# Twenty loads at the end of layer 1's attention begun by POOL in place of SP

## The chip, the cores and the metric

The program runs on one core of a Trainium2 chip. Its five engines each work through a queue of their own, in the order in which the program was built: PE (TensorE, matrix products), DVE (VectorE), ACT (ScalarE), POOL (GpSimd) and SP (SyncE, which here only begins transfers). Semaphores order the engines among each other. The metric is the device time of one execution in microseconds (us), given as the median of three runs.

## What is computed

Two decoder layers over 1024 positions of width 1024. Layer 1 ends its mixer part like this (cut from the reference):

```python
o_mix = forgetting_attention(q, k_sh, v_sh, dcum)      # 12 heads of 64
o_mem = memory_attention(q_mem, mem, mem_norm[l], w_mem_kv[l])   # 4 heads of 64
x = x + jnp.concatenate([o_mix, o_mem], axis=-1) @ w_o[l]        # 1024 x 1024
x = x + conv_ffn(rms_norm(x, ffn_norm[l]), w_up[l], conv_w[l], conv_b[l], w_down[l])
```

The change sits between the attention of layer 1 and the product with `w_o[1]`.

## The kernel before

Every large product is computed with two-part operands: a value is split into a rounded part (`hi`, written by ACT, line 173) and the rest (`lo`, written by DVE, line 174), and three products are summed (`mm3`, lines 249 to 251).

Layer 1's attention is written by `attention`. Its units are a head and a half `c` of the positions (512 of them). A unit's scores are made by PE (`score`, line 392, into `psa`), masked by DVE (line 422), exponentiated by ACT (line 435) and scaled by DVE (line 482). Then, step by step, PE turns 128-wide blocks (line 512, into `psb`), ACT and DVE split them into `pt` (lines 523 and 526), and PE multiplies them with the values (line 536). ACT copies the finished unit to `ob` (line 628) and SP stores it to the DRAM tensor `o` (line 630), both parts apart. Between these steps the projections of the queries and keys of later heads are computed; they read the layer's input from four `hT` buffers.

When both heads of a pair (`kt`, eight of them) are stored for one `c`, `operand` loads the pair's 128 rows of `o` (line 595), POOL adds the two parts (line 596), and ACT and DVE split the sum into `oT`, the left operand of the output projection. There are 16 operands. In the order of the program they are (c, kt) = (0,0), (1,0), (0,1), (1,1), (0,6), (1,6), (0,2), (1,2), (0,3), (1,3), (0,7), (1,7), (0,4), (1,4), (0,5), (1,5); "operand 7" below is the seventh of these. `oT` takes the four `hT` buffers, so no operand can be split before the projections have read their last input of that half. Once, at the start of the last unit, `load_block` loads the first half of the columns of `w_o[1]` in four pairs of `kt` (`load_rows`, line 282), each split into `wh` and `wl` (lines 173 and 174 again).

All these loads, 16 and 4, and the projections' weights before them, land in `wr`, which has three buffers: `wraw` gives the next one, and a load into it waits until the split of the one before has read it. Behind the attention `out_proj` runs over the columns in two halves `n` and the rows in eight tiles `t`; tiles 0 to 3 need the operands of c = 0, tiles 4 to 7 those of c = 1, and each takes `kt` in the order 0, 1, 2, 3, 4, 6, 7, 5. It accumulates in `psb`, of which there are four; DVE adds the sum to `x` (line 1290). The second half of `w_o[1]` is loaded there, by SP.

The order on each engine in layer 1's attention is made by a scheduler: it takes the operations by the order of the program, as their inputs and buffers come free by its own estimate of the times. So a transfer that is put on another queue also changes the order of the other engines. Once built, the order is fixed, and an engine whose next instruction waits does nothing else.

Of the kernel before, what the change touches and what calls it, by code (L numbers as in the profile page):

```python
# [18 lines left out]
P = 128  # L19
# [3 lines left out]
KT = D // P  # L23
CH = 512
# [15 lines left out]
def f32(ap):  # L40
    return ap.bitcast(F32)
# [93 lines left out]
class Trunk:  # L135
# [137 lines left out]
        self.split(raw, hi, lo)  # L273
        return lambda kt: (hi[:, kt, :], lo[:, kt, :])

    def load_rows(self, w, k0, nk, cols, gcol=None, pool=None):

        width = sum(n for _, n in cols)
        raw = self.wraw([P, nk, width])
        o = 0  # L280
        for c0, n in cols:
            self.nc.sync.dma_start(raw[:, :, o:o + n], w[k0 * P:(k0 + nk) * P, c0:c0 + n].rearrange("(k p) n -> p k n", p=P))
            o += n
        if pool is None:
            hi, lo = self.whl([P, nk, width])
        else:
            hi, lo = (self.sb(pool, [P, nk, width], F32R, n, KT // nk) for n in ("bh", "bl"))
        if gcol is None:
            self.split(raw, hi, lo)
        else:  # L290
            for k in range(nk):
                g = gcol[:, k0 + k:k0 + k + 1]
                self.nc.scalar.activation(hi[:, k, :], raw[:, k, :], AF.Identity, scale=g)
                self.nc.vector.scalar_tensor_tensor(lo[:, k, :], raw[:, k, :], g, f32(hi[:, k, :]), ALU.mult, ALU.subtract)
        return hi, lo

    def load_block(self, w, cols, gcol=None, step=2, pool=None):
        tiles = [self.load_rows(w, k0, min(step, KT - k0), cols, gcol, pool) for k0 in range(0, KT, step)]

        def at(kt, c0, n):  # L300
            hi, lo = tiles[kt // step]
            return hi[:, kt % step, c0:c0 + n], lo[:, kt % step, c0:c0 + n]
        return at
# [254 lines left out]
    def attention(self, ap, l, od, units, work, spare, lead=4, lag=2, lead_work=2):  # L558
# [30 lines left out]
        def operand():  # L589

            if not oT:
                oT.extend(self.hpair() for _ in range(2))
            c, kt = whole.pop(0)
            raw = self.wraw([P, 2, CH])
            self.nc.sync.dma_start(raw, od[c][:, kt * P:(kt + 1) * P, :].rearrange("s p q -> p s q"))
            self.nc.gpsimd.tensor_tensor(raw[:, 0], raw[:, 0], raw[:, 1], ALU.add)  # L596
            self.split(raw[:, 0], oT[c][0][:, kt, :], oT[c][1][:, kt, :])

# [3 lines left out]
        def run(k, slot):  # L602
            for f in later.pop((k, slot), ()):
                f()

        def advance():
            nonlocal total
            total -= 1
            if next(work[0][1], 0) == 0:
                done.add(work.pop(0)[0])  # L610

        def begin(k, it):
            if it["load"]:
                while not set(it["u"]["needs"]) <= done:
                    advance()
                it["u"]["load"]()
            self.score(it)
            after(k + 1, "max", lambda: self.maximum(ap, it))
            after(k + 1, "exp", lambda: self.exponent(ap, it))
            if "norm" in it:  # L620
                after(k + 2, "norm", lambda: self.normalise_all(it["u"], *it["norm"]))

        def finish(k, u):
            h, c = u["at"]

            def out():
                ot = self.sb(ap, [P, CH], F32, "ob", 2)
                self.nc.scalar.activation(ot, u["o"], AF.Copy)
                for i in range(2):
                    self.nc.sync.dma_start(od[c][i, h * HD:(h + 1) * HD, :], ot[i * HD:(i + 1) * HD, :])  # L630
                halves.append((c, h // 2))
                if halves.count((c, h // 2)) == 2:
                    whole.append((c, h // 2))
            after(k + 1, "exp", out)

        first = min(it["at"] for it in items)
        for k in range(first, len(steps) + lag + 4):
            st = steps[k] if 0 <= k < len(steps) else None
            run(k, "max")
            if st:  # L640
                self.turn_p(ap, st)
                self.upper_p(ap, st)
            run(k, "exp")
            if st:
                self.lower_p(st)
            run(k, "norm")
            while items and items[0]["at"] <= k:
                begin(k, items.pop(0))
            if k < 0 and lead_work and items:
                for _ in range(lead_work):  # L650
                    if work:
                        advance()
            if st and k < n_fill:
                owed += max(total, 0) / (n_fill - k)
                while owed >= 1 and work:
                    owed -= 1
                    advance()
            if 0 <= k - lag < len(steps):
                for part in range(len(steps[k - lag]["t"])):
                    self.value(steps[k - lag], part)  # L660
                if steps[k - lag]["end"]:
                    finish(k, steps[k - lag]["u"])
            if not work and whole and k % 4 == 0:
                operand()
            if k == units[-1]["start"]:
                w_o = self.load_block(self.a["w_o"][l], [(0, CH)])
        while whole:
            operand()
        assert not work and not later
# [1320 lines left out]
```

## Time and profile before

| | us |
|---|---|
| median of 3 runs | 2552.12 |
| lowest, highest | 2549.92, 2553.2 |
| profiled execution, its own time | 2546.43 |
| its span | 2544.6 |
| PE busy in the span | 2455.0 (96%) |
| DVE, ACT, POOL busy | 1823.9 (72%), 1340.3 (53%), 791.3 (31%) |

The profile is one execution. Its times count from the start of the span; 1.8 us of its own time lie outside. A line of the timeline has the start, the length, the engine, the line of the kernel, what is written from what, and, in brackets, how long the engine had been idle and what ended that. "SPq" is an issue on SP's queue: its length is that of the issue, not of the transfer. In the chain of waits, a "DMA" piece is the part of a transfer that the chain waited for. POOL's operations before layer 1's attention ended lie in other stages; from 1607 to 1845 us it does nothing but the 16 additions of line 596. The products of the first half `n` of the output projection begin at 1787.8 us.

### The profile page before, as it was taken

The numbers are of one execution on the slowest core, as the hardware profiler recorded it, in microseconds if no ns is written. First come the engines' busy times: TensorE is split into PE (matmuls) and PEld (weight loads), VectorE is DVE, ScalarE is ACT, GpSimd is POOL, SyncE is SP. The second block draws the span as 40 slices with busy tenths as digits, with TensorE's granted clock in tenths as the row PEclk, the third lists the DMA queues.
The fourth block names the chain that finished last, engine by engine and source line by source line (L and its number), as shares of the span: only waits on it lengthen the run. The fifth ranks groups of instructions, "written<-read, shape, count | busy, mean of one in ns | idle before, by whom it ended". The sixth has DMA issues, their size and how long they took to land.

```text
span 2544.6 us, 35639 instructions
## 1 busy us (share of the span) xinstructions
PE 2455.0 (96%) x12306; PEld 2052.6 (81%) x12306; DVE 1823.9 (72%) x3074; ACT 1340.3 (53%) x2553; POOL 791.3 (31%) x714
## 2 busy tenths in 40 slices
PE   7899999988999999999999999999999999999998
PEld 7788888776878888888889888887777888888886
DVE  5648787676477877879765468878476778778765
ACT  5338787686254544544454356767244444444443
POOL 1235555485135564540000000000234455551000
PEclk9999999999999999999999999999999999999999
DMA  8473333344323332358235467665622233238533
GB/s 248 140 218 91 92 109 104 88 140 158 118 76 103 104 111 96 104 182 290 93 124 165 144 182 203 188 180 176 221 89 87 94 106 112 95 104 307 170 95 115
DMA packets 302700, 357.68 MB, mean 141 GB/s; under 512 B 37960, under 2 KB 183224, under 8 KB 302520
## 3 DMA queue, kind: packets, MB, share of 16 engines
q1 hardware_dynamic: 302520, 355.41, 44.1%
q8 instruction: 97, 1.59, 0.3%
q14 instruction: 83, 0.68, 0.1%
HBM read 245.55 MB, written 109.78 MB: 140 GB/s over the span
## 4 chain that ended last, share of the span: by engine, by line
PE 79%; DVE 5%; ACT 4%; DMA 3%; POOL 2%; issue 2%; SPq 1%; POOLq 0%; ACTq 0%; DVEq 0%
PE psa L249 12%; PE psa L250 12%; PE psa L251 12%; PE psb L251 9%; PE psb L249 9%; PE psb L250 9%; PE psa L392 5%; PE psb L512 4%; PE psb L536 4%; ACT pt L523 1%; DVE pt L526 1%; ACT ps L435 1%; DVE ps L422 1%; DMA qq<-qd 1%; PE psb L1322 1%
## 5 line engine op out<-in xcount | busy, mean ns | idle before, releaser
L173 ACT ACTIVATE wh<-wr 128x512 fp32r<-128x512 f32 (+2 forms) x240 | 181.8, 761 | 311.4 <-PE psb L251 146.7
L1764 DVE SCALAR_TENSOR_TENSOR v<-u,cw,v 128x1023 f32<-128x1023 f32 (+1 forms) x176 | 275.2, 1564 | 68.7 <-ACT v L1762 68.5
L174 DVE TENSOR_TENSOR wl<-wr,wh 128x512 fp32r<-128x512 f32 (+2 forms) x232 | 222.9, 963 | 121.3 <-ACT wh L173 120.6
L526 DVE TENSOR_TENSOR pt<-psb,pt 128x512 fp32r<-128x512 f32 (+2 forms) x380 | 244.4, 660 | 70.0 <-ACT pt L523 68.6
L1762 ACT ACTIVATE v<-u,cw 128x1024 f32<-128x1024 f32 x88 | 109.6, 1245 | 310.0 <-DVE u L1751 296.9
L523 ACT ACTIVATE pt<-psb 128x512 fp32r<-128x512 f32 (+2 forms) x380 | 212.9, 575 | 106.2 <-PE psb L512 70.0
L536 PE MATMUL psb<-pt,vv 128*128 128x512 f32 (+2 forms) x864 | 244.0, 361 | 11.9 <-DVE pt L526 7.3
L213 POOL TENSOR_TENSOR rs<-ss,consts 128x1 f32<-128x1 f32 x44 | 25.5, 582 | 675.9 <-DVE ss L211 467.2
L249 PE MATMUL psa<-hT,wh 128*128 128x512 f32 x560 | 219.1, 392 | 5.3 <-DVE u L1725 5.3
L251 PE MATMUL psa<-hT,wl 128*128 128x512 f32 x560 | 218.5, 390 | 0.2 <-DVE wl L174 0.2
L250 PE MATMUL psa<-hT,wh 128*128 128x512 f32 x560 | 218.5, 390 | 0.0
L392 PE MATMUL psa<-kk,qq 128*128 128x512 f32 (+4 forms) x792 | 178.8, 344 | 16.0 <-DMA qq<-qd 5.0
L536 PEld LDWEIGHTS psb<-pt,vv 128*128 128x128 f32 x864 | 144.5, 190 | 33.0 <-DVE pt L526 12.5
L435 ACT ACTIVATE ps<-ps,stat 128x128 f32<-128x128 f32 (+1 forms) x192 | 147.3, 770 | 31.9 <-DVE stat L422 31.6
L422 DVE CUSTOM_DVE_ANT_0 ps<-psa,caub 128x128 f32<-128x128 f32 (+1 forms) x192 | 138.9, 751 | 32.5 <-PE psa L392 29.8
L249 PE MATMUL psb<-hT,wh 128*128 128x512 f32 x384 | 156.6, 408 | 1.2 <-ACT wh L173 0.9
L392 PEld LDWEIGHTS psa<-kk,qq 128*128 128x128 f32 x792 | 121.9, 192 | 38.7 <-DVE stat L422 14.7
L251 PE MATMUL psb<-hT,wl 128*128 128x512 f32 x384 | 151.8, 395 | 0.8 <-POOL wl L174 0.8
L250 PE MATMUL psb<-hT,wh 128*128 128x512 f32 x384 | 151.0, 393 | 0.0
L512 PE MATMUL psb<-consts,ps 128*128 128x128 f32 x928 | 146.6, 276 | 4.2 <-DVE pt L526 3.4
L596 POOL TENSOR_TENSOR wr<-wr 128x512 f32<-128x512 f32 x16 | 21.6, 1353 | 411.5 <-DMA kd<-st 243.7
L1666 POOL TENSOR_TENSOR ws<-wr 128x512 f32<-128x512 f32 x44 | 77.5, 1761 | 216.2 <-DMA wr<-in_w_up_dram 175.7
(310 smaller groups left out, 6830.3 us busy)
## 6 DMA issues: line engine op xcount, KB each, us to landing
wr<-in_w_up_dram SPq DMA_DIRECT2D x88, 512.0 KB
wr<-gd SPq DMA_DIRECT2D x154, 256.0 KB
gd<-v SPq DMA_DIRECT2D x88, 256.0 KB
gd<-gs SPq DMA_DIRECT2D x66, 256.0 KB
o<-ob SPq DMA_DIRECT2D x128, 128.0 KB
wr<-o SPq DMA_DIRECT2D x32, 512.0 KB
hT<-in_w_down_dram SPq DMA_DIRECT2D x64, 256.0 KB
qd<-st SPq DMA_DIRECT2D x56, 256.0 KB
```

Of the source, the lines that this page charges most:

```text
L173: nc.scalar.activation(hi, src, AF.Copy)
L174: (low or nc.vector).tensor_tensor(lo, src, f32(hi), ALU.subtract)
L249: mm(out, lh, rh, start=first, stop=False, skip_group_check=more)
L250: mm(out, lh, rl, start=False, stop=False, skip_group_check=more)
L251: mm(out, ll, rh, start=False, stop=last, skip_group_check=more)
L392: nc.tensor.matmul(out, w, rhs, start=b not in banks[:i], stop=b not in banks[i + 1:])
L435: nc.scalar.activation(p, p, AF.Exp, bias=st[:, 0, ii:ii + 1], scale=-1.0, accum_out=st[:, 1, ii:ii + 1])
L512: nc.tensor.transpose(tp[0:kb, x:x + P], br["pt"][ii][:, o:o + kb], self.ident)
L523: self.nc.scalar.activation(st["hi"], st["src"], AF.Copy)
L526: self.nc.vector.tensor_tensor(st["lo"], st["src"], f32(st["hi"]), ALU.subtract)
L536: self.nc.tensor.matmul(u["o"][:, iis[0] * P:iis[0] * P + w], br["v"](j), t[:, x:x + w], start=st["begin"] and first and i == 0, stop=st[" ...
L1764: nc.vector.scalar_tensor_tensor(v[:, d:], u[:, :S - d], cw[:, tap, i:i + 1], v[:, d:], ALU.mult, ALU.add)
```

## The change

`load_rows` and `load_block` take a queue, which is SP's if none is given. The operand loads and the four loads of the first half of `w_o[1]` are begun by POOL:

```diff
-    def load_rows(self, w, k0, nk, cols, gcol=None, pool=None):
+    def load_rows(self, w, k0, nk, cols, gcol=None, pool=None, queue=None):
...
-            self.nc.sync.dma_start(raw[:, :, o:o + n], w[k0 * P:(k0 + nk) * P, c0:c0 + n].rearrange("(k p) n -> p k n", p=P))
+            (queue or self.nc.sync).dma_start(raw[:, :, o:o + n], w[k0 * P:(k0 + nk) * P, c0:c0 + n].rearrange("(k p) n -> p k n", p=P))
...
-            self.nc.sync.dma_start(raw, od[c][:, kt * P:(kt + 1) * P, :].rearrange("s p q -> p s q"))
+            self.nc.gpsimd.dma_start(raw, od[c][:, kt * P:(kt + 1) * P, :].rearrange("s p q -> p s q"))
...
-                w_o = self.load_block(self.a["w_o"][l], [(0, CH)])
+                w_o = self.load_block(self.a["w_o"][l], [(0, CH)], queue=self.nc.gpsimd)
```

Nothing else is edited. On POOL, at the end of the attention, the loads now stand among the additions. The part from operand 6 (`wr_17468`) on, with the weight pairs (`wr_17485` to `wr_17503`) and operands 7 to 10 (`wr_17544`, `wr_17581`, `wr_17592`, `wr_17597`), lines with + are new on this engine:

```order
 L596 TENSOR_TENSOR wr_17468<-wr_17468 128x512
+L282 DMA wr_17491<-in_w_o_dram 128x2x512
+L282 DMA wr_17497<-in_w_o_dram 128x2x512
+L282 DMA wr_17503<-in_w_o_dram 128x2x512
+L595 DMA wr_17544<-o_0_13658 128x2x512
+L595 DMA wr_17581<-o_1_13659 128x2x512
 L596 TENSOR_TENSOR wr_17544<-wr_17544 128x512
+L595 DMA wr_17592<-o_0_13658 128x2x512
 L596 TENSOR_TENSOR wr_17581<-wr_17581 128x512
+L595 DMA wr_17597<-o_1_13659 128x2x512
 L596 TENSOR_TENSOR wr_17592<-wr_17592 128x512
```

Before, POOL had the additions alone. Now each load from operand 9 on stands behind the addition of the operand two places earlier; so it goes on to the end.

On ACT, the copies of operand 6 and of the first three weight pairs (`wh_17487`, `wh_17493`, `wh_17499`) move forward, among the softmax of a later unit (`ps_2736`):

```order
 L628 ACTIVATE ob_17145<-psb_17085 128x512
+L173 ACTIVATE hT_17090<-wr_17468 128x512
 L523 ACTIVATE pt_17170<-psb_17165 128x512
+L173 ACTIVATE wh_17487<-wr_17485 128x1024
 L523 ACTIVATE pt_17186<-psb_17181 128x512
 L523 ACTIVATE pt_17202<-psb_17197 128x512
+L173 ACTIVATE wh_17493<-wr_17491 128x1024
+L173 ACTIVATE wh_17499<-wr_17497 128x1024
+L435 ACTIVATE ps_2736_17135,stat_17134<-ps_2736_17135,stat_17134 128x640
+L435 ACTIVATE ps_2736_17135,stat_17134<-ps_2736_17135,stat_17134 128x768
 L523 ACTIVATE pt_17217<-psb_17214 128x256
```

Before, the copy of operand 6 stood some 30 rows later, ahead of the first weight pair's. Operand 5's copy (`hT_17088<-wr_17407`) moves in the same way, to the place ahead of `pt_17008`, a unit earlier.

On DVE, near the end of the attention, the split of the second weight pair (`wl_17494`) now stands where that of the first (`wl_17488`) stood:

```order
+L526 TENSOR_TENSOR pt_17458<-psb_17455,pt_17458 128x256
 L450 TENSOR_SCALAR stat_17338<-stat_17338 128x4
-L174 TENSOR_TENSOR wl_17488<-wr_17485,wh_17487 128x1024
+L174 TENSOR_TENSOR wl_17494<-wr_17491,wh_17493 128x1024
 L451 RECIPROCAL stat_17338<-stat_17338 128x4
-L526 TENSOR_TENSOR pt_17458<-psb_17455,pt_17458 128x256
+L174 TENSOR_TENSOR wl_17500<-wr_17497,wh_17499 128x1024
 L482 TENSOR_SCALAR ps_2777_17339<-ps_2777_17339,stat_17338 128x640
```

The first pair's and operand 6's splits have gone forward on this engine too, and the third pair's now stands ahead of the last unit's scalings, not behind them.

## Rows read from the trace of the kernel before

**Rows 1.** The page's first part: busy time, share, instructions of each engine.

```profile
PE 2455.0 (96%) x12306; PEld 2052.6 (81%) x12306; DVE 1823.9 (72%) x3074; ACT 1340.3 (53%) x2553; POOL 791.3 (31%) x714
```

**Rows 2.** Stretches: length, busy us of PE, PEld, DVE, ACT, POOL, clock, DMA, GB/s.

```profile
1740.00:1750.00 10.00, 9.42 (x60) 7.52 (x58) 9.36 (x25) 8.30 (x20) 0.00 (x0) 1.00 0.79 235
1750.00:1760.00 10.00, 9.38 (x54) 7.77 (x53) 8.70 (x24) 7.30 (x18) 1.29 (x1) 1.00 0.59 181
...
1770.00:1780.00 10.00, 6.78 (x35) 4.68 (x36) 9.56 (x19) 6.47 (x12) 0.00 (x0) 0.96 0.29 90
1780.00:1790.00 10.00, 8.70 (x36) 6.37 (x35) 9.04 (x12) 6.13 (x11) 2.59 (x2) 0.70 0.70 227
1790.00:1800.00 10.00, 9.58 (x41) 7.52 (x42) 2.90 (x4) 2.83 (x5) 5.18 (x4) 1.00 0.79 238
1800.00:1810.00 10.00, 8.28 (x36) 6.08 (x35) 3.83 (x6) 2.82 (x5) 6.11 (x4) 1.00 0.78 263
```

**Rows 3.** Whom PE waited for, 1600 to 1860: us in total, times, longest.

```profile
PE psb L536 <- DVE pt L526: 5.0, 8, 1.1
PE psb L249 <- ACT hT L173: 2.1, 3, 1.5
...
PE psa L392 <- DMA qq<-qd: 0.8, 1, 0.8
```

**Rows 4.** PE's timeline in the output projection (start, length, instruction, idle before).

```profile
1802.86 0.50 PE L249 MATMUL psb<-wh,hT 128*128 128x512 f32 x1 [1.48 <-ACT hT L173]
...
1807.06 0.50 PE L249 MATMUL psb<-wh,hT 128*128 128x512 f32 x1 [0.24 <-ACT hT L173]
```

**Rows 5.** The chain of waits that ended last, at the tail: start, length, what.

```profile
1792.23 4.67 DMA wr<-o
...
1800.20 3.42 DMA wr<-o
```

**Rows 6.** POOL's timeline: addition 7, and 14 with 15.

```profile
1785.71 1.30 POOL L596 TENSOR_TENSOR wr<-wr 128x512 f32<-128x512 f32 x1 [16.97 <-DMA wr<-o]
...
1803.75 2.59 POOL L596 TENSOR_TENSOR wr<-wr 128x512 f32<-128x512 f32 x2 [1.60 <-DMA wr<-o]
```

**Rows 7.** The page's third part: DMA queues, packets, MB, share of 16 engines.

```profile
q1 hardware_dynamic: 302520, 355.41, 44.1%
```

**Rows 8.** Line 595 alone: issue in ns (least, median, most), first and last start.

```profile
L595 SPq DMA_DIRECT2D wr<-o x16: 359/370/586, 1615.5 to 1803.6; - x16
```

**Rows 9.** SP's timeline: the issues of operands 7 to 10.

```profile
1780.84 9.14 SPq L595 DMA_DIRECT2D wr<-o x4
```

**Rows 10.** DVE's timeline: splits of operands and weights, a block, a burst of scalings.

```profile
1731.71 0.68 DVE L174 TENSOR_TENSOR hT<-wr,hT 128x512 fp32r<-128x512 f32 x1
...
1742.09 0.69 DVE L174 TENSOR_TENSOR hT<-wr,hT 128x512 fp32r<-128x512 f32 x1 [0.29 <-ACT hT L173]
...
1775.81 1.22 DVE L174 TENSOR_TENSOR wl<-wr,wh 128x1024 fp32r<-128x1024 f32 x1
...
1777.04 0.39 DVE L526 TENSOR_TENSOR pt<-psb,pt 128x256 fp32r<-128x256 f32 x1
1777.35 2.33 DVE L482 TENSOR_SCALAR ps<-ps,stat 128x640 f32<-128x640 f32 x4
1779.59 1.22 DVE L174 TENSOR_TENSOR wl<-wr,wh 128x1024 fp32r<-128x1024 f32 x1
...
1787.83 1.76 DVE L174 TENSOR_TENSOR hT<-wr,hT 128x512 fp32r<-128x512 f32 x1
```

**Rows 11.** ACT's timeline: what now stands behind a copy, and a weight pair's copy.

```profile
1737.97 0.60 ACT L523 ACTIVATE pt<-psb 128x512 fp32r<-128x512 f32 x1 [0.16 <-PE psb L512]
...
1748.43 1.27 ACT L523 ACTIVATE pt<-psb 128x512 fp32r<-128x512 f32 x2 [0.50 <-PE psb L512]
...
1753.88 0.82 ACT L435 ACTIVATE ps<-ps,stat 128x640 f32<-128x640 f32 x1
...
1772.97 1.05 ACT L173 ACTIVATE wh<-wr 128x1024 fp32r<-128x1024 f32 x1
```

## What I expect of it, and why

> **What bounds the kernel now.** The page's first part comes first: TensorE (PE) is busy for 96% of the span [rows 1], so a change gains only where PE waits, and loses wherever it makes PE wait. Then the stretches of ten microseconds around the place of the change [rows 2]: from 1740 to 1760 us PE is busy for 9.4 of 10, from 1770 to 1780 only for 6.78, from 1780 to 1790 its granted clock is 0.70 on the mean (1 is 2.4 GHz, 0.5 is 1.2), and until 1810 us it still has gaps. VectorE (DVE) is busy for 9.56 and 9.04 of 10 us from 1770 to 1790, so until then DVE sets the pace, not a transfer. The list of waits says the same [rows 3]: between 1600 and 1860 us PE waited 5.0 us for DVE's `pt` and 2.1 us, in three pieces, for ACT's `hT`, the operands of the output projection; its only wait for a transfer is 0.8 us for a `qq`, which is not among the transfers that move. The two larger pieces of the 2.1 us that matter are PE's stops before 1802.86 (1.48 us) and 1807.06 us (0.24) [rows 4], for the thirteenth and the fifteenth operand. After the second, PE has no gap to speak of for the rest of the first half of the projection. So the end of this stage is the arrival of operand 15; the chain of waits runs over two of the tail's loads [rows 5], POOL's additions [rows 6] and ACT's copy.
>
> **What the change removes.** 16 operand loads and 4 weight loads leave SP's queue. Since PE waited 0.8 us for a transfer in 260 us [rows 3], nothing late is freed by that: the stores and query loads that stood behind them were in time. I cost the emptier SP at nothing; what covers it is that PE and DVE are full there, and without that cover it is worth the 0.8 us.
>
> **What it adds: the loads on POOL.** All transfers of the kernel's data run over one hardware queue [rows 7], and no row shows one begun by POOL, so its price needs bounds. Below: SP's price, 0.37 us to issue [rows 8], and 3.42 us to landing, the faster of the two tail loads in the chain [rows 5]. Above: an issue as long as POOL's own addition over the same tile, 1.30 us [rows 6], and the slower landing plus the longer issue, 4.67 + 0.93 = 5.6 us. I take the middle of the issue, 0.83 us, and the middle of the landings (4.05 us) plus the 0.46 us by which the issue is longer: L = 4.5 us from the start of the issue to the data. A price below SP's own I leave out: the same bytes go over the same 16 engines.
>
> By the Trainium skill (DMA: Bandwidth & Descriptors, Latency and other measured facts) the first byte comes some 0.6 us after the start from the sync queue and some 1 us from POOL's; L would then be an estimated 4.45 us and the sum below 2.5 instead of 2.8 us. No run here shows it.
>
> **What it moves (1): the prefetch depth at the tail.** Before, SP issues an operand's load as soon as one of three buffers is free, so three are in flight, and a pair of additions takes 4.8 us: addition 7 starts at 1785.71 us, addition 15 ends at 1803.75 + 2.59 = 1806.34 us [rows 6]. After, loads and additions stand in one queue, and the order reads load n+1, addition n, load n+2, addition n+1. Load n+2 cannot begin before addition n is done, although its buffer may be free: two are in flight, not three. A pair then costs L + 1.3 us, 5.8 us at L = 4.5. From the end of addition 7 to that of addition 15 there are four pairs.
>
> **What it moves (2): where the tail begins.** Operand 7 takes the buffer of the second weight pair. Before, its load was issued at 1780.84 us [rows 9], when DVE's second `wl` had ended (1779.59 + 1.22) [rows 10]. After, operand 6 and the first weight pair stand earlier on DVE, and the second `wl` follows where the first stood: that ended at 1775.81 + 1.22 = 1777.03 us, then a `pt` of 0.39 and a `wl` of 1.22 give 1778.6 us [rows 10], 2.2 us earlier, if nothing before it is delayed.
>
> **What it moves (3): three places where ACT can now stand.** ACT and DVE work in a fixed order, and the new order puts copies of loads between the softmax work. Operand 5's load may go when DVE has split operand 3 (1731.71 + 0.68) [rows 10], at 1732.4 us; it lands at 1736.9, POOL adds operand 4 first (till 1737.2), then it (till 1738.5), ACT copies till 1739.15. The `pt` behind it started at 1737.97 us before [rows 11]: 1.2 us late. Operand 6 waits for operand 2's split, which ended at 1742.09 + 0.69 = 1742.78 [rows 10] and now near 1744.0; landed 1748.5, added 1749.8, copied 1750.4, while the `pt` behind it started at 1748.43 [rows 11]: 2.0 us late. The third weight pair takes operand 6's buffer (split by 1751.1), lands at 1755.6 us and is copied (1.05 us) by 1756.7; the exponential behind it started at 1753.88 [rows 11]: 2.8 us late, of which 2.1 us are two weight copies that only moved. This is one delay that grows, not three. DVE was idle for 0.64 + 1.30 = 1.9 us from 1740 to 1760 us [rows 2], which takes part of it. I take S = 1.5 us left at operand 7, and as ends 0 (POOL as quick as SP) and 3 us (all of the largest place).
>
> **The sum.** Addition 15 ends at 1778.6 + S + 5 x (L + 1.3). With S = 1.5 and L = 4.5 that is 1809.1 us against 1806.34: **2.8 us later**. PE then stands some 2 us more before operand 15, and the rest follows unchanged, since PE has no gap behind it to make it up. The profiled execution (2546.43 us, span 2544.6) would become 2549.2; the median of the runs is 2552.12, and the same 2.8 us on it give **2554.9 us**. Ends: L = 3.42 and S = 0 give 1802.2, 4.1 us earlier, of which PE can use the 2.1 us that it waited for operands and perhaps 2 more from DVE work that has left the full stretch: 2548. L = 5.6 and S = 3 give 1816.1, 9.8 us later: 2562.
>
> One row speaks for a further price. The split of operand 7 at 1787.83 us took DVE 1.76 us where others take 0.69 [rows 10], beside one of POOL's additions: the two engines hinder each other. The Trainium skill (SBUF — State Buffer, Who interferes with whom) states that POOL cannot write a transfer's descriptors while DVE runs an operation in a two-port mode, which `tensor_scalar`, the kernel's scaling by 1/sum, can enter. The scalings come in bursts of four, 2.33 us for the long ones [rows 10]. By that rule the third weight load, released just ahead of a burst of short ones, would come about half such a burst later, S would be some 1.2 us larger and the sum 4.0 us; without it, 2.8.
>
> **Rivals.** A difference of 0.2%, 5.1 us, is about what a measurement of this kernel can tell from no change.
> - *The POOL load is dear* (slower by over 0.2%). Place: the alternation of loads and additions at the tail. The sum rises by 5 us for each microsecond of L, and by S; 5.1 us are passed near L = 4.9 with S = 2, which is the slower landing with an issue of 0.6 us. It would give 2558 to 2562. For it: both upper ends are ordinary rows, and longer stops of PE may bring its clock down as after the gaps of 1770 to 1780 us; a stretch like that from 1780 to 1790 us costs up to 3 us [rows 2]. Against: the faster landing. Chance 0.33.
> - *The POOL load is as cheap as SP's and the earlier splits pay* (faster by over 0.2%). The 2.1 us of operand waits go, DVE is relieved of operand 6 and the first weight pair in its full stretch, and PE keeps its clock from 1780 to 1790 us (up to 3 us): 2547. For it: DVE is the bound there. Against: two in flight instead of three, and the work that left that stretch went into one that is nearly as full. Chance 0.08.
> - *It does not reach the end.* The order changes, but the earlier start pays for the slower pairs (L near 4.2, S near 1: 0.8 us later): 2552 to 2553. This belongs to "no change" with the forecast.
>
> **How the numbers follow.** The forecast with the third rival 0.59, the slower rival 0.33, the faster 0.08. The likeliest is the forecast, 2554.9. The range from 2548 to 2562 is that of the two ends of the sum and leaves about 0.1 on either side.
>
> **What would show it.** In the trace after: the length of POOL's row of a load (0.83 by me) and the time from its start to the addition (L). Additions 9, 11, 13 and 15 should be near 5.8 us apart, and PE's stop before operand 15 near 2 us where it was 0.24. ACT should stand before the copies of operands 5 and 6. The prediction is wrong if POOL's issue costs as little as SP's, if three loads turn out to be in flight, if DVE loses more than 3 us before 1770 us to the copies that now stand ahead, or if PE's clock from 1780 to 1790 us comes out otherwise, which no row of before decides.

## The result, and the profile after

The changed kernel takes 2567.64 us (median of 4 runs, 2567.15 to 2571.34), the kernel before 2551.02 (4 runs) beside it: a ratio of 1.0071 with an interval of 1.0060 to 1.0083, or 18 us of 2551 (the two medians alone are 16.6 us apart). The forecast was 2.8 us; the time lies above its range, 2548 to 2562. The profiled execution took 2571.34 us (span 2569.5), the slowest of the four; that of before, 2546.43 us, was a quick one.

Two executions cannot be compared by their clock times as they stand. The first row of line 628 (`ob<-psb`), at 1492.32 us before, starts at 1496.61 after, and the rows up to 1572 us keep that distance within 0.07 us. The first load that the change moves comes at 1615.5 us [rows 8], so 4.29 us is the distance between the two executions. **Late** below always means: later than the same row of before, less this distance, which is taken anew for each kernel. Up to the end of attention it is good to about 1.5 us: e11 below, whose order is that of before up to operand 6, is 0.5 us late at 1590 us and 1.6 at the end of attention. It compares single executions, and behind attention it differs from the measured times by up to 3.7 us (e7).

The stretches of ten microseconds of the kernel after, against [rows 2] (length; busy us of PE, PEld, DVE, ACT, POOL; clock; DMA share; GB/s):

```profile
1750.00:1760.00 10.00, 7.01 (x41) 5.16 (x41) 9.43 (x25) 7.36 (x18) 4.11 (x5) 1.00 0.83 257
1760.00:1770.00 10.00, 5.39 (x15) 4.18 (x16) 4.35 (x8) 4.88 (x9) 0.00 (x0) 0.70 0.68 191
...
1810.00:1820.00 10.00, 7.58 (x31) 5.91 (x30) 2.62 (x4) 1.89 (x3) 6.22 (x6) 0.93 0.84 256
1820.00:1830.00 10.00, 6.84 (x23) 5.06 (x23) 2.67 (x4) 1.26 (x2) 3.40 (x4) 0.84 1.02 407
```

Two holes are new. In the first, from 1750 to 1770 us, where PE was busy for 18.5 of 20 before, it is busy for 12.4, and the granted clock falls to 0.70 on the mean (0.5, the lower level, from 1764.5 to 1770). In the second, from 1810 to 1830, PE stands for 5.6 of 20 while the transfer engines fill up (0.84, then 1.02 and 407 GB/s). PE's stops from 1790 to 1810 us are for the most part those that before had from 1770 to 1790, moved along. Whom PE waited for from 1600 to 1880 us, against [rows 3]:

```profile
PE psb L249 <- ACT hT L173: 5.6, 2, 3.2
PE psa L392 <- DMA qq<-qd: 5.5, 2, 5.3
PE psb L536 <- DVE pt L526: 4.6, 5, 2.0
PE psb L512 <- DVE ps L482: 3.8, 4, 2.7
```

The wait for DVE's `pt`, the largest before, is no larger. Three grew: the one for an operand (`hT`), which the prediction spoke of, the one for a query (`qq`), which it had set aside with 0.8 us, and the one for DVE's scalings (`ps`, 0.3 before), which it did not price (more on that one with e10 and e13 below).

The query's story on SP's timeline (issues), after:

```profile
1749.51 3.24 SPq L1033 DMA_DIRECT2D qd<-st  x2
...
1755.01 3.97 SPq L1502 DMA_DIRECT2D qq<-qd  x2
```

POOL's, in the same microseconds:

```profile
1737.83 0.72 POOL L595 DMA_DIRECT2D wr<-o  x1 [81.71 <-DVE hT L174]
1739.03 0.72 POOL L595 DMA_DIRECT2D wr<-o  x1 [0.48 <-DVE hT L174]
...
1751.10 0.72 POOL L595 DMA_DIRECT2D wr<-o  x1 [4.26 <-ACT pt L523]
1752.07 0.72 POOL L282 DMA_DIRECT2D wr<-in_w_o_dram  x1 [0.25 <-DVE hT L174]
...
1756.82 0.73 POOL L282 DMA_DIRECT2D wr<-in_w_o_dram  x1
1758.67 0.72 POOL L282 DMA_DIRECT2D wr<-in_w_o_dram  x1 [1.12 <-DVE hT L174]
```

And PE's:

```profile
1764.43 1.62 PE L392 MATMUL psa<-kk,qq 128*128 128x512 f32 x4 [5.32 <-DMA qq<-qd]
```

The query is stored to DRAM by `qd<-st` and read back by `qq<-qd`; PE waits for it. Beside that pair POOL now moves operand 6 and three pairs of weights, 512 KB each. Before, SP began operand 6 and the first weights behind the queries and the stores (SP's timeline of before):

```profile
1763.43 0.59 SPq L595 DMA_DIRECT2D wr<-o  x1
1764.12 12.15 SPq L282 DMA_DIRECT2D wr<-in_w_o_dram  x3
```

The tail, SP's timeline of before and, in the second fence, of after (the eight loads of the residual rows, `x<-xd`, 512 KB each):

```profile
1800.20 3.72 SPq L595 DMA_DIRECT2D wr<-o  x3
...
1805.20 4.46 SPq L1519 DMA_DIRECT2D x<-xd  x8
```

```profile
1815.30 4.11 SPq L1519 DMA_DIRECT2D x<-xd  x8
```

POOL's loads of operands 14 to 16 and additions 14 and 15, after:

```profile
1814.95 0.72 POOL L595 DMA_DIRECT2D wr<-o  x1
...
1817.46 0.72 POOL L595 DMA_DIRECT2D wr<-o  x1
1820.61 1.27 POOL L596 TENSOR_TENSOR wr<-wr 128x512 f32<-128x512 f32 x1 [2.43 <-DMA wr<-o]
1821.83 0.72 POOL L595 DMA_DIRECT2D wr<-o  x1
1825.41 1.25 POOL L596 TENSOR_TENSOR wr<-wr 128x512 f32<-128x512 f32 x1 [2.86 <-DMA wr<-o]
```

Before, the residual loads stood in SP's queue behind operand 16's, and filled the transfer engines (1.03, 406 GB/s) from 1810 to 1820 us, when addition 15 was done. After, no operand load is left in that queue, and they start ahead of those of operands 15 and 16. The load of operand 15 takes from 1817.46 to 1825.41 us. Addition 15 ends at 1826.66, 16.0 us late against [rows 6].

### The profile page after: what moved, and what is told of

The parts are those of the page before. It is cut to its first block, busy times and chain, and to the rows that moved or that the text cites. A ratio compares the mean times of both kernels' runs of the same rounds, so it can differ in the third digit from the quotient of the medians.

```text
span 2569.5 us, 35650 instructions
## 1 busy us (share of the span) xinstructions
PE 2465.7 (96%) x12306; PEld 2061.6 (80%) x12306; DVE 1834.1 (71%) x3074; ACT 1340.7 (52%) x2553; POOL 804.4 (31%) x734
## 4 chain that ended last, share of the span: by engine, by line
PE 79%; DVE 5%; DMA 4%; ACT 4%; issue 2%; POOL 2%; SPq 0%; POOLq 0%; ACTq 0%; DVEq 0%
PE psa L249 12%; PE psa L250 12%; PE psa L251 12%; PE psb L249 9%; PE psb L251 9%; PE psb L250 9%; PE psa L392 5%; PE psb L536 4%; PE psb L512 4%; DVE pt L526 1%; ACT pt L523 1%; DVE ps L422 1%; ACT ps L435 1%; PE psb L1322 1%; DMA wr<-o 1%
## 5 line engine op out<-in xcount | busy, mean ns | idle before, releaser
L1764 DVE SCALAR_TENSOR_TENSOR v<-u,cw,v 128x1023 f32<-128x1023 f32 (+1 forms) x176 | 283.5, 1611 | 68.7 <-ACT v L1762 68.5
L536 PE MATMUL psb<-pt,vv 128*128 128x512 f32 (+2 forms) x864 | 243.5, 361 | 12.2 <-DVE pt L526 7.2
L536 PEld LDWEIGHTS psb<-pt,vv 128*128 128x128 f32 x864 | 144.9, 191 | 32.3 <-DVE pt L526 11.2
L249 PE MATMUL psa<-hx,wh 128*128 128x512 f32 x368 | 144.0, 392 | 0.4 <-ACT u L1754 0.4
L250 PE MATMUL psa<-hx,wh 128*128 128x512 f32 x368 | 143.7, 390 | 0.0
```

What stands on the lines that cost most here:

```text
L249: mm(out, lh, rh, start=first, stop=False, skip_group_check=more)
L250: mm(out, lh, rl, start=False, stop=False, skip_group_check=more)
L536: self.nc.tensor.matmul(u["o"][:, iis[0] * P:iis[0] * P + w], br["v"](j), t[:, x:x + w], start=st["begin"] and first and i == 0, stop=st[" ...
L1764: nc.vector.scalar_tensor_tensor(v[:, d:], u[:, :S - d], cw[:, tap, i:i + 1], v[:, d:], ALU.mult, ALU.add)
```

## The experiments

Each kernel was timed beside the kernel before on the same chip. "Time" is the ratio less one, times 2551 us, with its interval. "Attention ends" is how late the last row of line 628 starts, "addition 15" how late that addition ends; both come from one profiled execution, and are a guide to the place of a loss more than to its price.

| run | begun by POOL | time against before, us | attention ends | addition 15 |
|---|---|---|---|---|
| after | operands 1 to 16, weights | +18.1 (15.3 to 21.2) | 13.5 | 16.0 |
| e1 | operands 1 to 6, weights | +9.2 (6.1 to 12.2) | 13.4 | 11.7 |
| e2 | operands 7 to 16 | +8.4 (5.4 to 11.5) | 0.8 | 10.9 |
| e3 | operands 1 to 16 | +12.8 (9.7 to 15.8) | 8.8 | 13.4 |
| e4 | weights | +2.0 (-0.3 to 4.1) | 4.5 | 3.8 |
| e5 | all of after, residual | +13.3 (10.2 to 16.3) | 14.0 | 12.9 |
| e6 | operands 7 to 16, residual | +1.8 (-0.3 to 4.1) | 1.6 | 3.1 |
| e7 | residual | -0.5 (-2.8 to 2.0) | 0.3 | 3.2 |
| e9 | operands 1 to 3 | +1.5 (-1.0 to 3.8) | 3.6 | 4.8 |
| e10 | operands 4 to 6, weights | +8.9 (5.1 to 12.5) | 9.9 | 8.3 |
| e13 | operands 4 to 6 | +3.8 (1.5 to 6.4) | 4.0 | 3.5 |

Four kernels with another order of operands (e8, e11, e12, e14) stand further down.

**Halves by place (e1, e2).** In `operand`, on the changed kernel, with a counter of its calls; e2 has `> 6` and leaves the weights to SP:

```diff
-            c, kt = whole.pop(0)
+            c, kt = whole.pop(0); self.n_op = getattr(self, "n_op", 0) + 1
...
-            self.nc.gpsimd.dma_start(raw, od[c][:, kt * P:(kt + 1) * P, :].rearrange("s p q -> p s q"))
+            (self.nc.gpsimd if self.n_op <= 6 else self.nc.sync).dma_start(raw, od[c][:, kt * P:(kt + 1) * P, :].rearrange("s p q -> p s q"))
```

> Only the loads of operands 1 to 6 and of the four weight pairs are begun by POOL; operands 7 to 16 by SP as before. The order of ACT, DVE and POOL up to operand 6 is that of the changed kernel, the order of the tail that of the kernel before. Theory A (two separate losses: an early one, in which the copies of the moved loads stand in front of softmax work on ACT and DVE and the loads themselves stand beside the chain from the query store to the query load, so that PE waits some 5 us for a query and operand 7 is loaded 7 us late; and a tail one, in which loads and additions alternate in one queue): the early loss stays, the tail runs at before's 4.8 us for a pair of additions, the stop of PE for a query at 1764 us is there with 4 to 6 us; time 7 to 10 us above before. Rival B (only the tail loses): same as before within 2 us, and no stop for a query. Rival C (every transfer begun by POOL costs the same): half of the 16.6 us, 8 us, but spread, without the 5 us stop.

> Only the loads of operands 7 to 16 are begun by POOL; operands 1 to 6 and the weights by SP as before. Up to operand 6 the order is that of the kernel before. Theory A: no stop for a query, operand 7 loaded at before's time, then pairs of additions about 6.4 us apart as in the changed kernel instead of 4.8, 4 pairs: 6 us, and one or two more from the residual loads that the sync engine now begins earlier; time 6 to 9 us above before. Rival B (only the tail loses): 14 to 17 us above before, all of the loss. Rival D (only the early part loses): within 2 us of before.

Both halves lose, 9.2 and 8.4 us, and together 17.6 of the 18.1. So the loss is neither the tail alone nor the early part alone (rivals B and D fall). Rival C, the same price for every load on POOL, fits both times, 9 us for each half; e6 and e7 below decide it. e1 has the stop for a query, 3.92 us at 1761.27 us; its attention ends as late as that of the changed kernel.

e2 held the surprise. The first pairs of additions came 5.1 us apart, not 6.4; then POOL stood, here between additions 12 and 13:

```profile
1803.26 1.28 POOL L596 TENSOR_TENSOR wr<-wr 128x512 f32<-128x512 f32 x1 [0.59 <-DMA c<-in_conv_w_dram]
1804.49 0.73 POOL L595 DMA_DIRECT2D wr<-o  x1
1810.50 1.25 POOL L596 TENSOR_TENSOR wr<-wr 128x512 f32<-128x512 f32 x1 [5.28 <-DMA wr<-o]
```

PE's stop behind it in e2:

```profile
1812.47 0.80 PE L249 MATMUL psb<-wh,hT 128*128 128x512 f32 x1 [7.92 <-ACT hT L173]
```

And what SP had begun in e2 just ahead:

```profile
1799.77 5.05 SPq L1519 DMA_DIRECT2D x<-xd  x8
```

Here SP begins the residual loads at 1799.77 us, earlier still, in the middle of the tail. The theory was changed for it: not the alternation of loads and additions, but these 4 MB ahead of the last operands. That the time still fell into the expected 6 to 9 us was luck, since 6 of it were to come from the alternation.

**Halves by kind (e3, e4).** `load_block` without the new queue (e3), or `operand` on SP again (e4).

> All 16 operand loads are begun by POOL, the four weight loads by SP. Theory A: the weight loads no longer compete with the query's store and load and their copies stand late again, so the stop for a query shrinks to under 2 us; the tail's loss is whole: 7 to 11 us above before. Rival E (the weights that come early are the whole early loss and nothing else of it remains): exactly the tail's loss as in the run with operands 7 to 16 alone. Rival C (each transfer costs the same): 16 of 20 parts, 13 us above before.

> Only the four weight loads are begun by POOL, all operand loads by SP. The weights' copies stand on ACT and DVE within a few rows of where they were before. Theory A: nothing of the tail's loss, and little of the early one, since operands 5 and 6 are not in front: within 3 us of before. Rival E (the weight loads are the early loss): 6 us or more above before, with a stop of PE for a query. Rival C: 3 us above before.

The weights alone cost 2.0 us, with an interval that reaches zero, though attention ends 4.5 us late in their profile; the operands alone cost 12.8 us. In e3 the stop for a query before the scores near 1763 us is 0.39 us, where the changed kernel has 5.32: SP begins the first weights at 1765.08 there, behind the query loads. So the weights need the operands to do most of their harm. They land in the same three buffers, and only when operands 5 and 6 come early do the weights too. Rival C fitted e3 (13) and, within its interval, e4 (3) as well; the stops are where theory A put them. What was missed is e3's size, 12.8 where 7 to 11 stood: without that stop its attention still ends 8.8 us late.

**The residual loads put back behind the last operand (e5, e6), or put among the additions (e7).** One line, on the changed kernel, on e2, and on the kernel before:

```diff
-            self.nc.sync.dma_start(self.x[:, t, :], src[t * P:(t + 1) * P, :])
+            (self.nc.gpsimd if src is self.xd else self.nc.sync).dma_start(self.x[:, t, :], src[t * P:(t + 1) * P, :])
```

> The changed kernel, but the eight loads of the residual rows (x from xd, 512 KB each) are begun by POOL too, so that they stand behind the load of the last operand again, as they did in SP's queue before. Theory A2 (the tail loses because the sync engine, rid of the operand loads, begins the residual loads ahead of the last operands and they share the transfer engines): the last operands land in 4 to 5 us instead of 7.9, PE's stops for operands shrink, the time falls by 5 to 8 us against the changed kernel, to 9 to 12 us above before; what is left is the early loss. Rival F (the tail loses by the alternation of loads and additions in POOL's queue): within 2 us of the changed kernel, 15 to 18 us above before.

> Operands 7 to 16 begun by POOL, the rest by SP as before, and the residual loads by POOL behind the last operand. This leaves the alternation of loads and additions and takes the residual loads out of the tail. Theory A2: pairs of additions about 5.1 us apart to the end (4.8 before), stops of PE for operands 2 to 4 us together instead of 10.7; time 0 to 3 us above before. Rival F: 7 to 9 us above before, as with the residual loads on SP.

> The kernel before with one edit: the eight residual loads are begun by POOL. Operands and weights stay on SP. In POOL's queue six of the eight now stand between the last additions, so they start while the last operands are being loaded. Theory A2: the last four operands land 2 to 6 us later, PE stops for them; time 3 to 8 us above before, without any operand load on POOL. Rival F: within 2 us of before, since no operand load alternates with an addition.

e6 is the cleanest of all: operands 7 to 16 on POOL cost 8.4 us with the residual loads on SP and 1.8 with them behind, an interval that reaches zero. It also ends rival C, by which the 18 loads that POOL begins in e6 would cost 16 us and the 8 of e7 7; the runs show 1.8 and -0.5. Line 595 alone in e6 (issue in ns; transfers begun by POOL, from issue to landing):

```profile
L595 POOL DMA_DIRECT2D wr<-o x10: 722/723/958, 1787.0 to 1812.3; - x10
...
DMA to landing us min/median/max: 3.7/3.9/5.0
```

and in the changed kernel:

```profile
L595 POOL DMA_DIRECT2D wr<-o x16: 722/722/953, 1620.9 to 1821.8; - x16
...
DMA to landing us min/median/max: 3.6/5.1/7.9
```

Four pairs of additions, from the end of the seventh to that of the fifteenth, take 21.6 us in e6 (5.4 a pair), 25.7 in the changed kernel (6.4) and 19.3 before (4.8 [rows 6]). e5 gains 4.8 us on the changed kernel, a little under the 5 to 8 expected (13.3 above before, where 9 to 12 stood); its attention still ends 14.0 us late.

e7 missed. Two, one, two and one residual loads between the last additions make addition 15 3.2 us late, and PE stops 3.73 us for it (1.48 and 0.24 before [rows 4]), but the runs show no loss. So a few such loads spread out are borne; eight in one go ahead of operands are not.

**The early part taken apart (e9, e10, e13).** The same edit of `operand` with `<= 3` (e9, weights on SP) and `in (4, 5, 6)` (e10 with the weights on POOL, e13 with them on SP).

> Only the loads of operands 1 to 3 are begun by POOL; everything else by SP as before. On ACT and DVE the order of instructions is that of the kernel before, row for row; only the place of three loads among SP's changes. Theory A3 (a load that POOL begins is no longer behind the query loads in SP's queue, goes as soon as its buffer is free and shares the transfer engines with the query that PE wants next): operand 3's load starts near 1645 us, some 15 us earlier than before, PE stops 1.5 to 2.5 us for a query near 1650, the attention behind it runs 2 to 4 us late to its end; time 1 to 4 us above before. Rival G (the early loss comes from copies that stand in another place on ACT and DVE): no stop for a query, within 1 us of before in the profile at the end of attention.

> Operands 4 to 6 and the weights begun by POOL; operands 1 to 3 and the tail by SP. Theory A3: nothing is late at 1658 us; then the copy of operand 5, which stands ahead of softmax work, costs 2.5 to 5 us by 1747 us and the weight loads beside the query store and load 3.6 to 6.6 us by 1760; attention ends 8 to 11 us late, and the time is 6 to 9 us above before. With the run of operands 1 to 3 it adds up to the run of operands 1 to 6 with the weights (9.4 us) within 2 us. Rival G: the same total, but no stop of PE for a query near 1760.

> Operands 4 to 6 begun by POOL, all else by SP, the four weight loads too. The copies of operands 5 and 6 stand on ACT where the run with the weights on POOL has them; the weights' loads and copies stand late again. Theory A3 (of the early loss the weights' loads, which go beside the query's store and load, are the larger part): still 3 to 5 us late at 1747 us, no stop of PE for a query over 1 us behind it, the end of attention 2 to 5 us late; time 1 to 4 us above before. Rival G (the copies of the operands, in front of softmax work, are the larger part): 6 to 9 us above before, as with the weights.

In e9, ACT and DVE run the order of the kernel before, row for row, so what is late there is not order on these engines. POOL's load of operand 3, and PE:

```profile
1646.61 0.72 POOL L595 DMA_DIRECT2D wr<-o  x1 [9.46 <-DVE wl L294]
```

```profile
1652.61 0.97 PE L392 MATMUL psa<-ky,qx 128*128 128x512 f32 x4 [1.66 <-DMA qx<-qd]
```

Before, SP began that load at 1671.57 us, behind the queries. Begun 26 us earlier it stands beside the load of `qx`, and 3.3 us are lost from one row of line 628 to the next (0.5 late at 1647.67, 3.7 at 1657.88) and kept to the end of attention. Of that, the runs show 1.5 us, with an interval from -1.0 to 3.8: the mechanism is in the trace, its price in the time is not settled.

How late the rows of line 628 start that stand at these times in the kernel before:

| row before, us | after | e1 | e3 | e9 | e10 | e13 |
|---|---|---|---|---|---|---|
| 1647.67 | 0.6 | 0.8 | 1.8 | 0.5 | 0.1 | 0.9 |
| 1657.88 | 2.1 | 3.7 | 5.1 | 3.7 | -0.5 | 0.3 |
| 1742.96 | 2.6 | 4.8 | 6.4 | 3.7 | 1.5 | 2.9 |
| 1747.32 | 4.6 | 8.6 | 9.3 | 3.7 | 5.3 | 5.7 |
| 1760.40 | 11.2 | 12.2 | 9.1 | 3.7 | 8.4 | 5.7 |
| 1790.41 | 13.5 | 13.4 | 8.8 | 3.6 | 9.9 | 4.0 |

The step to 1657.88 comes with operands 1 to 3 (after, e1, e3, e9), as told. The step to 1747.32 comes with operands 4 to 6 on POOL, weights or not: the copy of operand 5 stands in front of softmax work on ACT, and operand 5's addition ends only when ACT has waited 2.71 us (ACT's timeline, after):

```profile
1746.87 0.63 ACT L173 ACTIVATE hT<-wr 128x512 fp32r<-128x512 f32 x1 [2.71 <-POOL wr L596]
```

PE then stops 2.0 us for a `pt`. The step to 1760.40 comes only with the weights on POOL as well (after, e1, e10), and it is the stop for the query. From the end of the stores' issue to the end of the queries' it is 6.2 us in the changed kernel, 6.3 in e10 and 4.7 in e1, and 3.8 in e13, where SP begins the weights behind the queries; of the four weight loads the three beside the queries land after 6.7 to 7.6 us, the fourth, at 1770.65 us, after 4.1. e10 costs 8.9 us and e13 3.8, and attention ends 9.9 and 4.0 us late: by the lateness the weights beside the query loads are the larger share, the operands' copies the smaller, as theory A3 had it. In the times the shares are 5.1 and 3.8 us, which their intervals do not tell apart. The weights' copies on ACT and DVE move with their loads, so the first share is that of both; the stop itself is for a transfer. e9 and e10 add up to 10.4 us, e1 is 9.2.

The last step, to 1790.41, has another place. At 1777.91 the changed kernel is 9.9 us late, then 13.5. DVE now runs the splits of two weight pairs ahead of the last unit's scalings, where before it ran one, and PE waits:

```profile
1794.72 2.79 PE L512 MATMUL psb<-consts,ps 128*128 128x128 f32 x12 [2.69 <-DVE ps L482]
```

The same wait is 2.7 to 3.0 us in e1, e3, e10 and e13, whose steps there are 1.7 to 3.2 us; it was 0.17 before, and e9, with the order of before, has a step of 0.1. No run takes this order apart from the rest.

**The operands of the first half first (e8, e11, e12, e14).** Rows 0 to 511 of the projection need only c = 0:

```diff
-            c, kt = whole.pop(0)
+            c, kt = whole.pop(min(range(len(whole)), key=lambda i: whole[i][0]))
```

e8 is the kernel before with it, e11 the kernel before with it from operand 7 on only; e12 and e14 are e5 and e6 with it from operand 7 on.

> The kernel before, but of the operands that are ready those of the first half of the rows go first, so that the last eight loads or so are for the second half, which PE needs some 22 us later. Theory A2 (the end of the stage is the arrival of the last operand of the first half): PE's 2.1 us of stops for operands vanish; time 1 to 4 us below before. If the copies that change place on ACT and DVE cost as much as in the changed kernel, it is 0 to 5 us above before.

> The kernel before; from operand 7 on, those of the first half of the rows go first (five of the first half, then five of the second). The order up to operand 6 is unchanged, so the attention ends at before's time (the version with the new order from operand 1 on ended it 3 us late). PE needs the last operand of the first half when addition 11 is done instead of addition 15, two pairs or 9 to 10 us earlier: the 2.1 us of stops for operands vanish and PE keeps its clock; time 3 to 7 us below before. If the operands are not what PE waits for at the end of the stage, within 1 us of before.

> The changed kernel with the residual loads behind the last operand, on POOL, and from operand 7 on those of the first half of the rows first. The early loss stays (13 to 14 us late at the end of attention in the profile), the tail's is gone: time 3 to 6 us below the changed kernel with the residual loads on POOL alone, 7 to 11 us above before. If the tail's remaining stops come from something other than the order of operands, within 2 us of that run, 13 us above before.

> Operands 7 to 16 begun by POOL, those of the first half of the rows first; the residual loads by POOL behind the last operand; operands 1 to 6 and the weights by SP as before. If a tail on POOL is free once the residual loads are behind it and the first half is first: no stop of PE for an operand over 1 us, attention ends within 2 us of before; time 1 to 5 us below before. If the alternation of loads and additions still costs: 0 to 2 us above before, as without the new order.

The stretches of e12:

```profile
1810.00:1820.00 10.00, 9.99 (x43) 7.25 (x42) 2.60 (x4) 2.49 (x4) 6.50 (x7) 1.00 0.72 200
1820.00:1830.00 10.00, 10.00 (x46) 8.29 (x45) 2.68 (x4) 2.53 (x4) 7.83 (x10) 1.00 0.80 254
1830.00:1840.00 10.00, 10.00 (x46) 8.29 (x45) 2.86 (x5) 0.00 (x0) 2.37 (x5) 1.00 1.03 399
```

With the residual loads behind and the first half first, PE is full there and has the full clock, where the changed kernel had its second hole; the residual loads fill the transfer engines from 1830 us on and hurt nobody. e12 is 8.7 us above before (5.9 to 11.5, expected 7 to 11), 4.6 below e5, although its attention ends 15.5 us late. What is left is the early part: e1 had 9.2. On the kernel before, the same order brought little: e8 -2.8 us (-5.4 to -0.3), e11 -2.0 (-4.6 to 0.3), e14 +1.3 (-1.3 to 3.6). PE still waited 2.0 us in e11 and 2.5 in e14 for operands, all of it before 1805 us, when the first half's had not all come; in e14 no stop over 1 us was expected, and the two took 1.43 and 1.09. So the expected 3 to 7 us for e11 was too much: with a tail that is not late, there is little to gain there. Of these e8 is the only one whose interval stays below before, by 0.01%; I would not call it settled.

## Why the prediction was wrong, point by point

- **"I cost the emptier SP at nothing"** is the step that failed, twice. SP's one queue was not only a place where transfers wait: its order was the order in which the transfer engines were given work. The prediction asked what had been late behind the loads (nothing), and not what the loads had been kept behind (the queries) or what they had kept back (the residual loads). Putting the residual loads behind again took the tail's cost from 8.4 to 1.8 us (e2, e6); leaving the weights behind the queries took e10's 8.9 us to 3.8 (e13). Both were to be read ahead: SP's order of before has operand 6 and the weights behind query loads, and the residual loads behind operand 16.
- **S, the delay before operand 7.** 1.5 us, at most 3. Operand 7's load starts at 1793.56 us, 1789.3 less the distance of the executions, against the 1778.6 of the working: S is 10.7. Of the three places named, ACT's wait before the copy of operand 5 is there: ACT idles 2.71 us and the row of 1747.32 loses 2.0, where 1.2 stood. The stop for the query, which is the largest, was not on the list, nor the early load of operand 3, nor PE's wait for the scalings. And a stop costs more than its length: the clock was 0.70 from 1760 to 1770 us. With the trace's numbers the sum closes: 10.7 for 1.5 in S, 6.1 for 4.5 us in operand 7's load, and 25.7 for 23.2 us in the four pairs are 13.2 us more, which with the 2.8 make the 16.0 of addition 15.
- **L, a POOL load.** 4.5 us, issue 0.83. The issue is 0.72. Undisturbed, as in e6 and e14, the load takes 3.9 and 4.0 us at the median, between the lower bound (3.42) and the 4.5; in the changed kernel 5.1, and 7.9 beside the residual loads. So the rival "the POOL load is dear" came out in the landing, but not by POOL: by what else was moved. Its time, 2558 to 2562, was passed too.
- **Two loads in flight, a pair costs L + 1.3.** Right as a mechanism: in e6 a pair takes 5.4 us, 3.9 + 1.3 = 5.2 by the formula. Over four pairs that is 2.3 us more than before; the runs show 1.8, which is not told apart from nothing.
- **"The rest follows unchanged."** No: addition 15 is 16.0 us late, the last row of line 1290 in this half 20.4. When PE goes on at 1827.38 us, 12 more products stand ahead of it than before at 1807.06, 2.7 us at 0.23 us each. And the eight from 1828.91 to 1832.32 us start 0.43 us apart, at the lower clock (0.50 from 1830 to 1832 us), which costs another 1.6; before, PE had the full clock there.
- **The rule on two-port operations of DVE** (the Trainium skill, SBUF — State Buffer, Who interferes with whom) was given 1.2 us. The rows of POOL's loads show nothing of it: they last from 0.72 to 0.96 us in every run. A wait within the landing is not ruled out. Operand 8's load landed after 5.8 to 6.2 us in the changed kernel, e5 and e12, beside a burst of four scalings, and after 4.8 to 4.9 in e2, e6 and e14, without one; but there operand 7's load also started 2.1 to 2.2 us ahead of it, not 1.2. No run tells the two apart.
- **What was right**: that the order would change, the place on ACT (operand 5's copy), and that nothing late was freed.

The Trainium skill (DMA: Bandwidth & Descriptors, Issuing engines are not separate DMA queues) says that transfers begun by different engines run on the same 16 engines and interleave, and that a second issuing engine saves only the time of the issue. The trace agrees: the 0.37 us that a load cost on SP [rows 8] became 0.72 on POOL, and loads begun by both at once took 7.9 us for 3.9.

What stays open is how much of the 18 us is clock and how much is waiting, since every long stop of PE brought both. The profiles set a bound: from 1600 to 1880 us the clock falls short of 1 by 10.2 us in sum after and by 3.4 before (one less the mean clock of each ten microseconds), so in these two at most 6.8 us are clock. Open too is what operand 3's early load, and DVE's order at the last scalings, cost in the runs.

## What to carry to other kernels

Before moving transfers to another queue, write down what stands ahead of them and what stands behind them in the queue they leave: the first they will now compete with, the second they no longer hold back. A queue that is never late may be so because of its order. And look for the buffers: here the weights came early only because the operands, which use the same three, did.

## What the runs showed of the hardware

- A load of 512 KB begun by POOL took 0.72 us of POOL and landed 3.7 to 5.0 us after its issue when little else moved (e6), hardly later than SP's 3.42 to 4.67 us in the chain [rows 5].
- Such a load did not wait for what SP's queue held: operand 3's was begun 26 us earlier in e9 than SP had begun it, and landed after 5.6 us; PE stood 1.66 us for a query load of 128 KB beside it.
- Eight loads of 512 KB in one go filled the transfer engines at 407 GB/s for ten microseconds and doubled the landing of two operands (7.9 us each); six of them spread over 12 us (e7) cost no time that the runs show.
- At the lower granted clock (0.50, 1.2 GHz) PE's products of 128x512 started 0.43 us apart, at the full one 0.23; it came behind PE's stops, of 5.32 us at 1764.43 and of 3.16 us at 1827.38.
